# The memory's norm weights move from eight transposed blocks per row tile to the rows themselves

## The chip, the cores and the metric

The kernel runs on one core of a Trainium2 chip. The metric is the time of one execution on the device, in microseconds (us); "PE" is TensorE, "DVE" VectorE, "ACT" ScalarE, "POOL" GpSimd and "SP" SyncE, which issues most of the transfers here.

## The reference, cut to what matters

One step of a two-layer streaming encoder on 512 prompt tokens and 64 sample tokens, 1024 wide. Each layer has one input projection, three mixers side by side (stick-breaking attention, gated linear attention, latent attention), an output projection, a cross-attention into 256 memory tokens, and a feed-forward part. The change is in how the prompt's memory becomes keys and values, once per layer:

```python
def rmsnorm(x, g):
    xf = x.astype(jnp.float32)
    y = xf * lax.rsqrt(jnp.mean(xf * xf, axis=-1, keepdims=True) + NORM_EPS)
    return (y * g.astype(jnp.float32)).astype(x.dtype)

def memory_kv(mem, w):
    B, M, _ = mem.shape                              # 1, 256, 1024
    h = rmsnorm(mem, w['g_mem_norm'])
    k = rmsnorm((h @ w['w_ck']).reshape(B, M, MEM_HEADS, MEM_HD), w['g_ckn'])
    v = (h @ w['w_cv']).reshape(B, M, MEM_HEADS, MEM_HD)
    return k, v
```

## The kernel before

**Precision.** Every large product is made of three matmuls on a rounded high part and a low part of each operand (a = aH + aL, with aH the value rounded to fp32r and aL the rest): aH bH + aL bH + aH bL. Making the two parts of a block costs one rounding copy, nearly always on ACT, and one subtraction on DVE (`split_to`). So each 128x1024 piece of weights costs ACT and DVE an instruction each, and so does each block of activations.

**Stages of a layer.** The names in the profile carry a stage and the layer: `win0` is the input projection, `gla0`, `sb0` and `mlaq0`/`mlak0`/`mlap0`/`mlas0` are the gated linear, the stick-breaking and the latent attention, `wout0` holds the memory's keys and values and the output projection, `cross0` and `ffn0` follow. The stage around the change runs from about 124 to 260 us in layer 0 and from 969 to 1105 us in layer 1.

**What sets the order of the work.** Inside this stage the order of the instructions on each engine is not written out. The pieces of work are Python generators in `Order` (L732 to L797). `Order.run` picks the next piece by its rank among those whose inputs are due by a modelled clock (`Clock`, L39 to L176); attention units have rank 0, and the long projection groups ("D" groups, mostly of 24 matmuls) rank 10, so that they fill the time for which an attention unit's softmax work is modelled to last. `Clock.cost` (L89) gives each instruction a modelled length; on DVE it is, for n elements per partition,

```python
            if op in ("tensor_scalar", "tensor_copy", "memset") and not psum:
                return 0.07 + n / 1920
            return 0.07 + n / 960 + (0.06 if op == "scalar_tensor_tensor" else 0.0)
```

A change in the instructions of one piece thus moves other pieces too. Once written, the order on each engine is fixed: an instruction waits for the one ahead of it on its engine and for its inputs.

**An attention unit.** A stick-breaking unit of a 128-token tile (`tile_attention`) makes scores on PE (`sb0.S`), two exponential-type passes per head on ACT into `sb0.kp` and `sb0.sg`, masks on POOL, on DVE a running sum (scan) in `sb0.kp` and a combination into `sb0.sg` per head, then transposes on PE (`sb0.T<-ident,sb0.sg`), copies of those to `sb0.PT` (one head's on ACT, the other's on DVE), and the product with the values on PE (`sb0.T<-sb0.PT,win0.sbv`). The units of the third and fourth token tile and of the sample come two each. A latent query unit (`mlaq0`) is a projection, a chain of small DVE, ACT and POOL instructions (`mlaq0.j`, `mlaq0.s`), and a transpose.

**The memory.** `memory_norm` (L800) loads 256 rows as two 128x1024 tiles (`wout0.mem`), takes the sum of squares on ACT (`wout0.mj` is its unused output), forms 1/rms (`wout0.s`) and scales each tile by it, with one DVE instruction per tile. `memory_turn` (L813) transposes the sixteen 128x128 blocks on PE, four into one PSUM bank. The norm's weight is now one number per partition, since a partition is one of the 1024 features, so each block is scaled as it is split: one ACT instruction into `wout0.mH` and one DVE instruction into `wout0.mL`, 128x128 each. The weights lie in `gT`, a small table of all gains that is loaded as rows (`grow`, L339) and transposed at the start. `memory_kv` (L830) then multiplies by the key and value weights, eight D groups of 24 matmuls (`wout0.D` with 256 columns). The transposes, the scores' transposes and other small things share one ring of three PSUM banks (`T`).

Of the kernel before, what the change touches and what calls it, by code (L numbers as in the profile page):

```python
# [20 lines left out]
D = 1024  # L21
# [195 lines left out]
def tile_hybrid(ctx, tc, ins, outs):  # L217
    clock = tc.clock = Clock()
    nc = Engines(tc)
    I = ins  # L220
# [15 lines left out]
    def nm(s):  # L236
        uid[0] += 1
        return f"{phase[0]}.{s}_{uid[0]}"

    def big(dt=F32, name="b"):  # L240
        return clock.tile(bp.tile([128, BIGN], dt, tag="big", name=nm(name)), "big", 11)
# [20 lines left out]
    def pt4(name="pt"):  # L262
        return clock.tile(turn["pool"].tile([128, 1024], F32, tag="pt", name=nm(name), bufs=2), "pt", 2)

    def small(n, tag="s"):
        bufs = {"s": 8, "y": 4}.get(tag, 1)
        return clock.tile(sp.tile([128, 16 if tag == "y" else 8], F32, tag=tag, name=nm(tag), bufs=bufs), tag, bufs)[:, :n]
# [4 lines left out]
    def ps_(tag):  # L272
        return clock.tile(pp.tile([128, 512], F32, tag=tag, name=nm(tag), bufs=PB[tag]), tag, PB[tag])

    def cst(shape, name, dt=F32):
        return const.tile(shape, dt, tag=name, name=name)
# [6 lines left out]
    def act(out, in_, func, **kw):  # L283
        name = TABLES.get(func)
        if name is not None and name != held["set"]:
            load = nc.scalar.preload_act_table_set(name).ins
            for i in held["users"]:
                behind(tc, load, i)
            held.update(set=name, load=load, users=[load])
        ins = nc.scalar.activation(out, in_, func, **kw).ins  # L290
        if name is not None:
            behind(tc, ins, held["load"])
            held["users"].append(ins)

    def copyA(out, in_, scale=None):
        if scale is None:
            act(out, in_, AF.Copy)
        else:
            act(out, in_, AF.Identity, scale=scale)

    def tt(out, a, b, op, eng=None):
        (eng or nc.vector).tensor_tensor(out, a, b, op=op)

    def stt(out, a, s, b, op0, op1):
        nc.vector.scalar_tensor_tensor(out, a, s, b, op0=op0, op1=op1)

    MUL, ADD, SUB = ALU.mult, ALU.add, ALU.subtract
# [18 lines left out]
    for t, (c0, n) in enumerate(TILES):  # L326
        if t == 3:
            w_first = fetch_w(I["w_in"][0, :, 768:1024], KD, 256)
        raw = big(name="xin")[:, 0:D]
# [6 lines left out]
    nc.chain.update(act=None, dve=None, pool=None)  # L336
    grow = u("kp", "grow")[0:84, 0:128]
    nc.vector.memset(grow, 1.0)
    for r0, g in ((16, "g_cross_norm"), (32, "g_ffn_norm"), (48, "g_mem_norm")):  # L339
        nc.pool_queue.dma_start(grow[r0:r0 + 16, :], I[g].rearrange("l (r c) -> (l r) c", c=128))  # L340
    nc.pool_queue.dma_start(grow[64:68, :], I["g_cq"].rearrange("l (r c) -> (l r) c", c=128))
    nc.pool_queue.dma_start(grow[68:70, :], I["b_gla_gate"])
# [38 lines left out]
    def rstd_small(ss, inv_n):  # L381
        nc.vector.tensor_scalar(ss, ss, inv_n, EPS, op0=MUL, op1=ADD)
        rows, n = ss.shape[0], ss.shape[1]
        nc.gpsimd.tensor_tensor(ss, ss, mhalf[0:rows, 0:n], op=ALU.pow)
# [49 lines left out]
    def tr(out, in_):  # L434
        n = in_.shape[0]
        nc.tensor.transpose(out, in_, ident[0:n, 0:n])
# [16 lines left out]
    def split_to(src, H, L):  # L453
        copyA(H, src)
        tt(L, src, H, SUB)
# [202 lines left out]
    gT = cst([128, 84], "gT")  # L658
# [44 lines left out]
    for t, (c0, n) in enumerate(TILES):  # L703
        if t < 3:
            x_squares(t, n)
        for i in range(0, KD, 4):
            d = ps_("DTS"[(2 * t + i // 4) % 3])
# [92 lines left out]
    def memory_norm(l, out):  # L800

        out["raw"] = big(name="mem")
        for t in range(2):
            raw, junk = out["raw"][:, t * 1024:(t + 1) * 1024], pt4("mj")
            nc.sync.dma_start(raw, I["mem_prompt"][0, t * 128:(t + 1) * 128, :])
            ss = small(1)
            act(junk, raw, AF.Square, accum_out=ss)
            rstd_small(ss, 1.0 / D)
            nc.vector.tensor_scalar(raw, raw, ss, None, op0=MUL)
        return  # L810
        yield

    def memory_turn(l, out):  # L813

        H = out["H"] = big(F32R, "mH")[:, 0:KD * MEM].rearrange("p (k c) -> p k c", c=MEM)
        L = out["L"] = big(F32R, "mL")[:, 0:KD * MEM].rearrange("p (k c) -> p k c", c=MEM)
        for t in range(2):
            for i in range(0, KD, 4):
                d = ps_("T")
                for j in range(4):  # L820
                    c = t * 1024 + (i + j) * 128
                    tr(d[:, j * 128:(j + 1) * 128], out["raw"][:, c:c + 128])
                for j in range(4):
                    g = gT[:, 48 + 8 * l + i + j:49 + 8 * l + i + j]
                    cs = slice(t * 128, (t + 1) * 128)
                    copyA(H[:, i + j, cs], d[:, j * 128:(j + 1) * 128], scale=g)
                    stt(L[:, i + j, cs], d[:, j * 128:(j + 1) * 128], g, H[:, i + j, cs], MUL, SUB)
                yield "T"

    def memory_kv(l, out, od):  # L830
# [67 lines left out]
    def layer(l, xn):  # L898
# [617 lines left out]
        if l == 0:  # L1516
# [15 lines left out]
        od.line([(["kv", "mlan"], mlas(p), None) for p in range(4)], 4, name="mlas")  # L1532
        phase[0] = f"wout{l}"
        od.line([(["glan"], memory_norm(l, mem), "mem")], 1, tag="T")
        od.line([(["mem"], memory_turn(l, mem), "memt")], 1, 0, tag="T")
        od.line([(["win", "memt"], memory_kv(l, mem, od), "memx"), (["gla", "win"], wout("gla", 256, 2), "wo1"),
                 (["sbn"], wout("sb", 0, 2), "wo0"), (["mlan"], wout("mla", 512, 4), None)], 1, 10, tag="D")
# [235 lines left out]
```

## Time and profile before

| | before |
|---|---|
| time, median of 3 runs (lowest to highest) | 1716.88 us (1714.28 to 1719.4) |
| the profiled execution's own time | 1715.26 us |
| its span | 1713.5 us |
| PE busy | 1649.6 us, 96% of the span |
| DVE busy | 1230.8 us, 72% |
| ACT busy | 903.9 us, 53% |
| mean granted clock of PE | 0.99 |

The span is what the profile covers; the execution's own time is 1.76 us more. Busy is the time in which an engine executes something. Every instruction stands under one line, L195, the helper that records them all, so groups are told apart by the names of what they write and read: `wout0.mL<-wout0.T,gT,wout0.mH` writes `wout0.mL` from a PSUM bank of the ring `T`, the gains and `wout0.mH`.

### The profile page before, as it was taken

To read this page: it belongs to the slowest core of one execution; us is meant where nothing else is said; L and a number is where in the kernel's file an instruction comes from. 1 tells how busy PE (TensorE), PEld (TensorE's weight loads), DVE (VectorE), ACT (ScalarE), POOL (GpSimd) and SP (SyncE) were. 2 spreads that over 40 slices of the span, in tenths; PEclk is the share of its full clock that TensorE was granted. 3 is DMA by queue.
4 is the path that set the end of the run, shared out by engine and by line. 5 is a ranking of instruction groups with operands and counts; after the bars stand their busy time and mean duration, and the time that the engine had idled before them with its cause. 6 is when DMAs were issued, how large, how long until landed. Compare 5 with 4: busy or idle time off the path is not lost.

```text
span 1713.5 us, 30864 instructions
## 1 busy us (share of the span) xinstructions
PE 1649.6 (96%) x12231; PEld 1532.3 (89%) x12231; DVE 1230.8 (72%) x2496; ACT 903.9 (53%) x1929; POOL 206.8 (12%) x303
## 2 busy tenths in 40 slices
PE   8999999999899999999999989999998999999998
PEld 7887887789889999999998978877897999999998
DVE  5737798776898677766657378987669986766763
ACT  6426688655654444344343456886666544334431
POOL 4323341020000000000134042400200000000000
PEclk9999999999999999999998999999999999999999
DMA  5321130022022322222222213200211233233221
GB/s 165 112 72 58 64 116 26 26 74 75 25 80 93 99 80 93 99 85 89 79 83 84 81 47 98 82 26 25 99 50 50 75 99 99 74 99 99 77 97 56
DMA packets 113647, 133.30 MB, mean 78 GB/s; under 512 B 10610, under 2 KB 95712, under 8 KB 113504
## 3 DMA queue, kind: packets, MB, share of 16 engines
q1 hardware_dynamic: 113120, 131.30, 24.2%
q8 instruction: 96, 1.57, 0.4%
q14 instruction: 47, 0.39, 0.1%
q0 software_dynamic: 352, 0.03, 0.0%
q10 hardware_dynamic: 32, 0.01, 0.0%
HBM read 123.64 MB, written 7.68 MB: 77 GB/s over the span
## 4 chain that ended last, share of the span: by engine, by line
PE 76%; DVE 13%; ACT 4%; issue 3%; POOL 2%; DMA 0%; POOLq 0%; ACTq 0%; DVEq 0%
PE ffn1.D L195 9%; PE ffn0.D L195 9%; PE ffn1.S L195 6%; PE ffn1.T L195 6%; PE ffn0.S L195 6%; PE ffn0.T L195 6%; PE win1.D L195 5%; PE win0.D L195 4%; PE cross0.D L195 3%; PE cross1.D L195 3%; PE wout1.D L195 2%; PE wout0.D L195 2%; PE cross0.T L195 1%; PE cross1.T L195 1%; PE mlap1.T L195 1%
## 5 line engine op out<-in xcount | busy, mean ns | idle before, releaser
L195 ACT ACTIVATE ffn1.wH<-ffn1.wraw 128x1024 fp32r<-128x1024 f32 x66 | 60.6, 918 | 115.8 <-PE ffn1.T L195 61.5
L195 ACT ACTIVATE ffn0.wH<-ffn0.wraw 128x1024 fp32r<-128x1024 f32 x66 | 60.6, 918 | 110.5 <-PE ffn0.T L195 60.0
L195 DVE TENSOR_TENSOR ffn1.sL<-ffn1.sum,ffn1.sH 128x1024 fp32r<-128x1024 f32 x44 | 53.7, 1221 | 40.3 <-ACT ffn1.sH L195 40.3
L195 DVE TENSOR_TENSOR ffn0.sL<-ffn0.sum,ffn0.sH 128x1024 fp32r<-128x1024 f32 x44 | 53.7, 1221 | 39.9 <-ACT ffn0.sH L195 39.8
L195 PE MATMUL ffn0.D<-cross0.bT,ffn0.sH 128*128 128x288 f32 x352 | 72.4, 297 | 2.4 <-ACT ffn0.sH L195 1.5
L195 PE MATMUL ffn1.D<-cross1.bT,ffn1.sH 128*128 128x288 f32 x352 | 73.1, 299 | 1.5 <-ACT ffn1.sH L195 0.9
L195 DVE TENSOR_TENSOR ffn0.wL<-ffn0.wraw,ffn0.wH 128x1024 fp32r<-128x1024 f32 x66 | 68.8, 1043 | 7.8 <-ACT ffn0.wH L195 7.2
L195 DVE TENSOR_TENSOR ffn1.wL<-ffn1.wraw,ffn1.wH 128x1024 fp32r<-128x1024 f32 x66 | 68.8, 1043 | 7.8 <-ACT ffn1.wH L195 7.3
L195 PE MATMUL ffn1.S<-cross1.bT,ffn1.sH 128*128 128x288 f32 x352 | 72.6, 297 | 1.0 <-ACT cross1.bT L195 0.5
L195 PE MATMUL ffn0.S<-cross0.bT,ffn0.sH 128*128 128x288 f32 x352 | 71.9, 294 | 0.8 <-ACT cross0.bT L195 0.5
L195 POOL TENSOR_TENSOR ffn0.u<-ffn0.u,ffn0.u 128x576 f32<-128x576 f32 x6 | 10.0, 1664 | 469.5 <-DVE ffn0.wL L195 462.5
L195 ACT ACTIVATE ffn1.sH<-ffn1.sum 128x1024 fp32r<-128x1024 f32 x44 | 46.3, 1055 | 27.1 <-PE ffn1.S L195 22.9
L195 PEld LDWEIGHTS ffn0.D<-cross0.bT,ffn0.sH 128*128 128x128 f32 x352 | 56.7, 189 | 4.0 <-ACT ffn0.sH L195 1.9
L195 ACT ACTIVATE ffn0.sH<-ffn0.sum 128x1024 fp32r<-128x1024 f32 x44 | 46.3, 1055 | 26.0 <-PE ffn0.S L195 22.8
L195 PEld LDWEIGHTS ffn1.D<-cross1.bT,ffn1.sH 128*128 128x128 f32 x352 | 57.3, 191 | 2.9 <-ACT ffn1.sH L195 1.3
L195 PEld LDWEIGHTS ffn1.S<-cross1.bT,ffn1.sH 128*128 128x128 f32 x352 | 57.6, 191 | 1.7 <-ACT cross1.bT L195 0.8
L195 PEld LDWEIGHTS ffn0.S<-cross0.bT,ffn0.sH 128*128 128x128 f32 x352 | 57.0, 189 | 1.4 <-ACT cross0.bT L195 0.8
L195 PE MATMUL ffn1.D<-cross1.bT,ffn1.sL 128*128 128x288 f32 x176 | 52.6, 299 | 0.0
L195 PE MATMUL ffn1.S<-cross1.bT,ffn1.sL 128*128 128x288 f32 x176 | 52.5, 299 | 0.0
L195 PE MATMUL ffn0.D<-cross0.bT,ffn0.sL 128*128 128x288 f32 x176 | 52.4, 298 | 0.0
L195 PE MATMUL ffn0.S<-cross0.bT,ffn0.sL 128*128 128x288 f32 x176 | 52.2, 297 | 0.0
L195 ACT ACTIVATE ffn0.part<-ffn0.D 128x288 f32<-128x288 f32 x66 | 26.9, 408 | 41.7 <-PE ffn0.D L195 41.7
(875 smaller groups left out, 6458.6 us busy)
## 6 DMA issues: line engine op xcount, KB each, us to landing
ffn0.wraw<-in_w_gate_dram SPq DMA_DIRECT2D x11, 1024.0 KB, 5.3
ffn0.wraw<-in_w_up_dram SPq DMA_DIRECT2D x11, 1024.0 KB, 5.5
ffn0.wraw<-in_w_down_dram SPq DMA_DIRECT2D x11, 1024.0 KB, 5.0
ffn1.wraw<-in_w_gate_dram SPq DMA_DIRECT2D x11, 1024.0 KB, 5.3
ffn1.wraw<-in_w_up_dram SPq DMA_DIRECT2D x11, 1024.0 KB, 5.4
ffn1.wraw<-in_w_down_dram SPq DMA_DIRECT2D x11, 1024.0 KB, 5.0
win1.wraw<-in_w_in_dram SPq DMA_DIRECT2D x7, 1024.0 KB, 5.3
win0.wraw<-in_w_in_dram SPq DMA_DIRECT2D x6, 1024.0 KB, 5.7
```

The source lines that it names most:

```text
L195: r = fn(*args, **kw)
```

## The change

The norm's weights are loaded per layer as one row broadcast over 128 partitions (`mg`, 128x1024), and applied to the memory's rows in the instruction that applies 1/rms. That instruction now has two tensor inputs. After the transposing nothing is left to scale, so the four blocks of a bank are split at once: one rounding copy on ACT and one subtraction on DVE, 128x4x128 each. The weights' load into `grow` goes.

```diff
-    for r0, g in ((16, "g_cross_norm"), (32, "g_ffn_norm"), (48, "g_mem_norm")):
+    for r0, g in ((16, "g_cross_norm"), (32, "g_ffn_norm")):
         nc.pool_queue.dma_start(grow[r0:r0 + 16, :], I[g].rearrange("l (r c) -> (l r) c", c=128))
...
         out["raw"] = big(name="mem")
+        gb = pt4("mg")
+        nc.sync.dma_start(gb, I["g_mem_norm"][l:l + 1, :].broadcast_to([128, D]))
         for t in range(2):
...
             rstd_small(ss, 1.0 / D)
-            nc.vector.tensor_scalar(raw, raw, ss, None, op0=MUL)
+            stt(raw, raw, ss, gb, MUL, MUL)
...
-                for j in range(4):
-                    g = gT[:, 48 + 8 * l + i + j:49 + 8 * l + i + j]
-                    cs = slice(t * 128, (t + 1) * 128)
-                    copyA(H[:, i + j, cs], d[:, j * 128:(j + 1) * 128], scale=g)
-                    stt(L[:, i + j, cs], d[:, j * 128:(j + 1) * 128], g, H[:, i + j, cs], MUL, SUB)
+                cs = slice(t * 128, (t + 1) * 128)
+                split_to(d.rearrange("p (k c) -> p k c", c=128), H[:, i:i + 4, cs], L[:, i:i + 4, cs])
```

The function that it calls is there already:

```python
    def split_to(src, H, L):
        copyA(H, src)
        tt(L, src, H, SUB)
```

Since `Order.run` works by the modelled lengths, the order of the whole stage comes out another way, in both layers alike. Three places show it.

On DVE, from the scaling of the second memory tile to the first stick-breaking scans (`win0.wL` are low parts of input weights, `win0.G` a gate; a scan stands here as a SCALAR_TENSOR_TENSOR on `sb0.kp`); first before, then the change:

```order
L195 TENSOR_SCALAR wout0.mem_1490<-wout0.mem_1490,wout0.s_1500 128x1024
L195 SCALAR_TENSOR_TENSOR win0.G_282<-win0.G_282,gT,gla0.u_1454 128x576
L195 SCALAR_TENSOR_TENSOR wout0.mL_1506<-wout0.T_1507,gT,wout0.mH_1505 128x128
L195 TENSOR_TENSOR win0.wL_1554<-win0.wraw_1547,win0.wH_1553 128x1024
L195 SCALAR_TENSOR_TENSOR wout0.mL_1506<-wout0.T_1507,gT,wout0.mH_1505 128x128
L195 TENSOR_TENSOR win0.wL_1825<-win0.wraw_1822,win0.wH_1824 128x1024
```

```order
L195 SCALAR_TENSOR_TENSOR wout0.mem_1489<-wout0.mem_1489,wout0.s_1501,wout0.mg_1490 128x1024
L195 SCALAR_TENSOR_TENSOR win0.G_281<-win0.G_281,gT,gla0.u_1453 128x576
L195 TENSOR_TENSOR wout0.mL_1507<-wout0.T_1508,wout0.mH_1506 128x4x128
L195 TENSOR_TENSOR win0.wL_1549<-win0.wraw_1542,win0.wH_1548 128x1024
L195 TENSOR_TENSOR win0.wL_1802<-win0.wraw_1799,win0.wH_1801 128x1024
L195 TENSOR_TENSOR win0.G_281<-win0.D_1552,in.R_140 128x288
```

One subtraction stands where four stood, and they no longer alternate with the 128x1024 subtractions.

On PE, at the third group of memory transposes, between the scores of the second token tile and its successor's filler; first before, then the change:

```order
L195 MATMUL sb0.S_1671<-win0.sbk_278,win0.qo_276 128x256
L195 MATMUL sb0.S_1671<-win0.sbk_278,win0.qo_277 128x256
L195 MATMUL sb0.T_1686<-ident,sb0.sg_1591 128x128 x2
L195 MATMUL sb0.T_1690<-ident,sb0.sg_1605 128x128 x2
L195 MATMUL wout0.T_1694<-ident,wout0.mem_1490 128x128 x4
L195 MATMUL win0.D_1707<-in.hH_135,win0.wH_1553 128x288
```

```order
L195 MATMUL sb0.S_1660<-win0.sbk_277,win0.qo_275 128x256
L195 MATMUL sb0.S_1660<-win0.sbk_277,win0.qo_276 128x256
L195 MATMUL wout0.T_1674<-ident,wout0.mem_1489 128x128 x4
L195 MATMUL sb0.T_1682<-ident,sb0.sg_1593 128x128 x2
L195 MATMUL sb0.T_1686<-ident,sb0.sg_1607 128x128 x2
L195 MATMUL win0.D_1690<-in.hH_134,win0.wH_1548 128x288
```

The memory's transposes move ahead of the unit's two; at the fourth group they move from behind the third tile's first scores to ahead of them.

On PE, behind the scores of the first unit of the third token tile (128x384) and one D group of 24 (its last row is the first here); first before, then the change:

```order
L195 MATMUL win0.D_1832<-win0.wH_1828,in.hL_138 128x256
L195 MATMUL sb0.T_1796<-sb0.PT_1795,win0.sbv_279 64x128 x8
L195 MATMUL sb0.S_1874<-win0.sbk_278,win0.qo_277 128x384
L195 MATMUL sb0.S_1886<-win0.sbk_278,win0.qo_277 128x384
L195 MATMUL sb0.T_1899<-ident,sb0.sg_1774 128x128 x3
L195 MATMUL sb0.T_1904<-ident,sb0.sg_1786 128x128 x3
L195 MATMUL win0.T_1909<-ident,win0.j_1857 128x128 x2
L195 MATMUL win0.D_1916<-win0.wH_1824,in.hH_135 128x256
```

```order
L195 MATMUL win0.D_1809<-win0.wH_1805,in.hL_137 128x256
L195 MATMUL sb0.T_1842<-ident,sb0.sg_1764 128x128 x3
L195 MATMUL sb0.T_1847<-ident,sb0.sg_1776 128x128 x3
L195 MATMUL sb0.T_1786<-sb0.PT_1785,win0.sbv_278 64x128 x8
L195 MATMUL sb0.S_1862<-win0.sbk_277,win0.qo_276 128x384
L195 MATMUL sb0.S_1874<-win0.sbk_277,win0.qo_276 128x384
L195 MATMUL sb0.T_1842<-sb0.PT_1841,win0.sbv_278 64x128 x6
L195 MATMUL win0.T_1893<-ident,win0.j_1834 128x128 x2
L195 MATMUL sb0.S_1900<-win0.sbk_277,win0.qo_275 128x512
L195 MATMUL sb0.S_1912<-win0.sbk_277,win0.qo_275 128x512
L195 MATMUL win0.D_1924<-win0.wH_1801,in.hH_134 128x256
```

The unit's transposes come sooner behind its scores, its product with the values follows with only the next unit's scores in between, and the next tile's scores stand ahead of the next D group instead of behind it. Through the rest of the stick-breaking units it goes on so: they end with one D group of the memory's keys and values among them where five stood, and the other four stand among the latent query and key units instead.

## Rows read from the trace of the kernel before

**Rows 1.** Windows: busy us (x count) of PE, PEld, DVE, ACT, POOL; clock; DMA.

```profile
124.00:260.00 136.00, 124.89 (x959) 109.79 (x959) 105.50 (x276) 94.82 (x239) 47.83 (x84) 0.99 0.25 83
969.00:1105.00 136.00, 124.21 (x965) 108.80 (x964) 105.53 (x274) 94.48 (x239) 48.12 (x84) 1.00 0.26 83
```

**Rows 2.** What PE waited for, 124 to 260 us: total us, times, longest us.

```profile
PE mlaq0.T L195 <- POOL mlaq0.j L195: 3.6, 6, 1.5
PE sb0.T L195 <- DVE sb0.PT L195: 2.6, 2, 1.9
PE win0.T L195 <- DVE sb0.PT L195: 1.4, 1, 1.4
PE wout0.T L195 <- DVE wout0.mL L195: 1.0, 1, 1.0
PE wout0.T L195 <- ACT win0.qo L195: 1.0, 1, 1.0
PE sb0.T L195 <- DVE wout0.mL L195: 0.4, 1, 0.4
```

**Rows 3.** The same from 969 to 1105 us.

```profile
PE wout1.T L195 <- DVE wout1.mL L195: 1.0, 1, 1.0
```

**Rows 4.** Tile `wout0.mH`, ns min/median/max, first and last start; who waited.

```profile
L195 ACT ACTIVATE wout0.mH<-wout0.T,gT x16: 349/367/417, 134.4 to 165.0; 128x128 fp32r<-128x128 f32 x16
L195 DVE SCALAR_TENSOR_TENSOR wout0.mL<-wout0.T,gT,wout0.mH x16: 319/344/352, 134.8 to 166.1; 128x128 fp32r<-128x128 f32 x16
...
  ACT wout0.mH L195: 12.7, 8
```

**Rows 5.** Timeline of PE: start, us, instruction, [idle before].

```profile
157.84 0.36 PE L195 MATMUL win0.D<-win0.wH,in.hH 128*128 128x256 f32 x1
...
160.89 0.43 PE L195 MATMUL sb0.T<-sb0.PT,win0.sbv 128*64 128x128 f32 x2
163.18 1.09 PE L195 MATMUL sb0.T<-sb0.PT,win0.sbv 128*64 128x128 f32 x14 [1.86 <-DVE sb0.PT L195]
```

**Rows 6.** Timeline of DVE, the same place.

```profile
159.42 2.18 DVE L195 TENSOR_TENSOR_SCAN sb0.kp<-sb0.kp,zero 128x384 f32<-128x384 f32 x2
...
162.44 0.68 DVE L195 COPY sb0.PT<-sb0.T 128x512 f32<-128x512 f32 x1
```

**Rows 7.** Window of 10 us, columns as in rows 1.

```profile
160.00:170.00 10.00, 8.14 (x58) 6.52 (x57) 7.79 (x16) 4.36 (x14) 3.44 (x7) 0.83 0.01 2
```

**Rows 8.** Groups by shape on ACT, 124 to 260 us: busy us, mean ns.

```profile
L195 ACT ACTIVATE sb0.PT<-sb0.T 128x512 f32<-128x512 f32 x3 | 1.9, 623 | 0.0
```

**Rows 9.** The same on DVE.

```profile
L195 DVE TENSOR_TENSOR wout0.wL<-wout0.wraw,wout0.wH 128x1024 fp32r<-128x1024 f32 x11 | 13.4, 1217 | 2.5 <-ACT wout0.wH L195 2.4
...
L195 DVE TENSOR_TENSOR X<-X,wout0.D 128x288 f32<-128x288 f32 x11 | 4.7, 445 | 0.6 <-PE wout0.D L195 0.6
...
L195 DVE COPY sb0.PT<-sb0.T 128x512 f32<-128x512 f32 x5 | 3.4, 677 | 0.3 <-PE sb0.T L195 0.3
...
L195 DVE SCALAR_TENSOR_TENSOR win0.G<-win0.G,gT,gla0.u 128x576 f32<-128x576 f32 x2 | 1.6, 814 | 0.7 <-ACT gla0.u L195 0.7
```

**Rows 10.** Tile `wout0.mem`.

```profile
L195 DVE TENSOR_SCALAR wout0.mem<-wout0.mem,wout0.s x2: 752/752/753, 129.2 to 133.0; 128x1024 f32<-128x1024 f32 x2
...
DMA to landing us min/median/max: 3.7/4.1/4.5
```

**Rows 11.** Timeline of SP, 85 to 101 us.

```profile
93.14 1.57 SPq L195 DMA_DIRECT2D out_dram<-gla0.s  x2
```

**Rows 12.** Timeline of PE, one unit of the fourth tile.

```profile
171.35 1.13 PE L195 MATMUL sb0.S<-win0.sbk,win0.qo 64*128 64x512 f32 x4
```

**Rows 13.** Timeline of DVE, the same unit.

```profile
174.91 0.76 DVE L195 TENSOR_TENSOR sb0.sg<-sb0.sg,sb0.kp 128x511 f32<-128x511 f32 x1
175.59 1.30 DVE L195 TENSOR_TENSOR_SCAN sb0.kp<-sb0.kp,zero 128x512 f32<-128x512 f32 x1
...
177.27 0.68 DVE L195 TENSOR_TENSOR sb0.sg<-sb0.sg,sb0.kp 128x511 f32<-128x511 f32 x1
```

## The prediction

> **What bounds the kernel now.** I read the windows by stage first, then the waits of PE inside the stage that the change touches, then the two tiles that it makes in another way. In the windows [rows 1], after the stretch and its length, PE is busy 124.89 of 136 us in layer 0 and 124.21 in layer 1: some 11 to 12 us per layer are idle PE, and no more than that can be won, since the change leaves the matmuls as they are. DVE has 105.5 us of work there and ACT 94.8; neither is full, but their work comes in bursts between which PE has to have something else to do. The waits [rows 2] say what PE stood still for: 2.4 us of it is at the memory's turning (1.0 for `wout0.mL`, 1.0 for a bank behind `win0.qo`, 0.4 for a unit's transposes behind `wout0.mL`), 4.0 us for copies of stick-breaking weights (2.6 and 1.4 for `sb0.PT` on DVE), and 3.6 us for the latent queries. Layer 1 repeats them, as its 1.0 us on `wout1.mL` shows [rows 3]. So 2.4 us per layer hang on the edited lines, and 7.6 us on units that the change only moves.
>
> **The work removed and added.** Per layer ACT has sixteen roundings of 0.367 us, 5.9 us, and DVE sixteen subtractions of 0.344 us, 5.5 us; the roundings waited 12.7 us, eight times, behind those subtractions [rows 4], which is nothing on PE by itself but keeps a PSUM bank of the ring of three in use. In the change four ACT copies of 512 elements take their place; the nearest row, a copy of 512 from PSUM, is 0.623 us [rows 8], so 2.5 us: ACT gains 3.4 us. The four subtractions of 512 from PSUM stand in no row. They lie between 0.445 us (288 elements from PSUM) and 1.217 us (1024 elements in SBUF), and a one-source copy of 512 from PSUM took 0.677 us [rows 9]; a line through the first two gives 0.445 + 224 x (1.217 - 0.445)/736 = 0.68, so I take 0.68, four of them 2.7 us. DVE gains 2.8 us there, and between 0.6 and 3.7 by the bounds.
>
> Against that, the scaling of the rows gets a second tensor. Before it is 0.752 us for 1024 elements [rows 10]. The same kind of instruction with two tensors took 0.814 us for 576; at the slope of the line above 1024 make 0.814 + 448 x 0.00105 = 1.28 us. Its floor is that 0.814, and its ceiling twice it, 1.63. Two per layer cost DVE 1.06 us more (0.1 to 1.8). DVE's net gain is 2.8 - 1.06 = 1.8 us per layer (between -1.2 and +3.6).
>
> [...]
>
> **The new load.** `mg` is 512 KB per layer on SP's queue. A memory tile of that size landed in 4.1 us [rows 10]. In the changed order it stands between the two stores of `gla0.s`, which were issued from 93.1 us on [rows 11], and the first scaling that needs it was at 129.2 us [rows 10]: 36 us of cover, so I cost it at nothing; without the cover it would be 4.1 us. Behind it on SP stand the second of those stores and the stores of `win0.kn`, for which nobody waits. It takes one of two buffers of the ring that `mj` and the weights' copies share, until the second scaling; the first stick-breaking copies stand behind it in the order. The gain's row that is no longer loaded on POOL's queue at the start is on no wait of PE: nothing.
>
> **What the new order does.** The PE waits at the memory go: one copy and one subtraction free a bank that eight instructions held, and the last two groups of transposes come ahead of unit transposes rather than behind them. I take all of it, -2.4 us per layer.
>
> The stick-breaking units get closer. In the change the first unit of the third tile has eight transposes and one D group between its scores and its own transposes. A D group of 24 took from 157.84 to 160.89, 3.05 us [rows 5], and eight transposes at that pace 1.0, so 4.05 us; its second head is wanted three transposes later, at 4.4. What a unit needs is shown by one of the fourth tile: scores from 171.35 to some 172.4 [rows 12], the first head's combination done at 175.67, the second's at 177.95 [rows 13], or 3.3 and 5.5 us after the scores, with a copy in between. With scans of 1.09 us [rows 6] instead of 1.30 and as much off the other steps it is some 4.8 for 384 elements; a gate product of about 0.8 us (the 0.814 of [rows 9]) that the new order puts between makes it 5.6. That gives a wait of 1.2 us. The two sample units have again one D group and eight small matmuls, 4.05 us, against 5.5: 1.5 us each, 3.0. Three products with the values come with only another product and scores between, some 1.7 us after their transposes (0.6 for eight matmuls at the pace of the 14 in [rows 5], 1.13 for scores [rows 12]), where a copy of 0.68 can stand behind a scan of 1.30: 1.98 - 1.7 is some 0.2 each, 0.6. The second unit of the third tile and those of the fourth have a second D group or a whole unit more between: nothing. Together 4.8 us in place of the 4.0 for `sb0.PT`: +0.8 us per layer. Its bounds are 0 (the D groups cover all of it), a gain of 4.0, and the second rival below.
>
> The four D groups that leave the stick-breaking units stand among the latent queries and keys. There they could cover part of the 3.6 us [rows 2], or be missed later; I take zero, with that 3.6 as the bound on both sides. [...]
>
> **The sum.** Per layer -2.4 + 0.8 = -1.6 us, which is near the 1.8 that DVE gains; twice, -3.2 us. From the execution of 1715.26 that is 1712.1 us; the runs' median stands 1.6 higher, at 1716.88, so I predict 1713.7 us, with 1711.7 to 1716 as this case's own range. 0.3%, or 5.15 us, is about what a measurement of this kernel can tell from no change, and the forecast lies inside it.
>
> **Rival: a larger gain.** If the D groups among the latent queries cover a quarter of their 3.6 us (0.9), and the unit waits that I count with 4.8 are half as long (2.4), a layer gains 2.4 + 4.0 - 2.4 + 0.9 = 4.9 us; two layers and the 1.7 us at the slow clock make 11.5: 1705.4 us. For it: DVE and ACT together lose 5.2 us of work per layer in a stage where PE's idle time is bursts of theirs, and banks come free sooner. Against it: the closer units.
>
> **Rival: slower.** The order is made with modelled lengths, and a scan of 512 elements, priced with 0.07 + 0.06 + 512/960 = 0.66 us, took 1.30 [rows 13]. Two heads make 1.3 us per unit that the order does not know of, and before it was D groups in plenty behind the scores that covered it. If all six units of the third and fourth tile and the sample come too early by 1.3 us, the waits are 7.8 + 0.6 = 8.4 us in place of 6.4, +2.0 per layer, and with a stretch of slow clock (1.7) in layer 1 as well, +5.7: 1722.6 us. It decides from 1.5 us of wait per unit on (9.0 against 6.4, twice).
>
> **Rival: no effect.** ACT and DVE are idle for 30 to 40 us per layer in this stage [rows 1]; the waits at the memory only move to the next unit behind, since each unit's chain ends when it ended: 1716.9 us.
>
> **How the numbers follow.** Forecast 0.35, larger gain 0.34, no effect 0.17, slower 0.14. The larger gain counts as faster by over 0.3%, and so do 0.02 of the forecast: 0.36. The rest of the forecast and no effect are 0.50, slower 0.14. The range reaches from 1704 us, the larger gain with some more of the 3.6 us, to 1721, which leaves out the worst half of the slower case and the tail beyond the larger gain.
>
> **What would show it.** Right: four `mL` instructions of 0.6 to 0.75 us, two `mem` scalings of 1.2 to 1.35, DVE 1.5 to 2 us less busy per layer in the stage, no PE wait for `mL`, and PE waits for `sb0.sg` of 1 to 1.5 us at the third tile's first unit and the sample's. Wrong: PE waits of 2 us or more at every unit, a wait for `mg`, latent-query waits far from 3.6 us, or a slow clock in other places.

## The result, and the profile after

The changed kernel takes 1730.73 us (median of 4 runs, 1726.22 to 1731.65) against 1716.12 for the kernel before: 1.0072 times as long, with a 95% interval of 1.0054 to 1.009. It is slower by 0.7%, outside the range I gave, and beyond the 1722.6 us of the slower rival. The profiled execution is the quickest of the four, 1726.22 us with a span of 1724.5 and a mean clock of 0.989. The other three have 0.985 to 0.987, so the profile below shows 11 of the 14.6 us and not all of them.

The windows of [rows 1] in the changed kernel:

```profile
124.00:260.00 136.00, 123.13 (x922) 105.33 (x921) 100.27 (x259) 91.41 (x232) 51.65 (x85) 0.99 0.25 81
969.00:1105.00 136.00, 123.66 (x935) 106.27 (x935) 96.23 (x243) 88.00 (x218) 49.93 (x83) 0.99 0.23 75
```

In layer 0 DVE and ACT are busy for 5.2 and 3.4 us less than before, and PE not for longer but for 1.8 us less. Part of that is work that now comes later: the window holds 922 matmuls, where it held 959. POOL is busy for longer, though the change gives it no work. A stretch with the same work in both kernels reaches from the last matmul of the gated linear attention to the last of the cross-attention (columns as in [rows 1]; first before, then the change):

```profile
130.06:467.76 337.70, 319.72 (x2362) 275.48 (x2362) 260.88 (x672) 229.76 (x601) 61.08 (x100) 0.99 0.18 58
975.74:1312.29 336.55, 317.82 (x2363) 273.69 (x2363) 260.70 (x673) 229.67 (x600) 61.38 (x100) 0.99 0.18 59
```

```profile
130.37:473.15 342.78, 323.08 (x2364) 275.60 (x2363) 259.24 (x661) 225.30 (x589) 64.03 (x100) 0.99 0.18 58
980.71:1323.23 342.52, 323.14 (x2363) 275.33 (x2363) 258.71 (x661) 225.66 (x589) 63.00 (x100) 0.99 0.18 58
```

Here DVE is busy for 1.6 and 2.0 us less per layer, as forecast, and the stretch is 5.1 and 6.0 us longer: all of the 11 us lie in it. What the new instructions cost, by tile (ns min/median/max):

```profile
L195 ACT ACTIVATE wout0.mH<-wout0.T x4: 577/594/622, 134.7 to 155.4; 128x512 fp32r<-128x512 f32 x4
L195 DVE TENSOR_TENSOR wout0.mL<-wout0.T,wout0.mH x4: 659/687/691, 135.3 to 156.3; 128x512 fp32r<-128x512 f32 x4
...
L195 DVE SCALAR_TENSOR_TENSOR wout0.mem<-wout0.mem,wout0.s,wout0.mg x2: 1285/1286/1287, 129.3 to 133.3; 128x1024 f32<-128x1024 f32 x2
...
L195 SPq DMA_DIRECT2D wout0.mg<-in_g_mem_norm_dram x1: 1262/1262/1262, 93.9 to 93.9; - x1
```

These are the prices of the prediction: 0.69 us (0.68), 1.29 (1.28), and a load issued at 93.9 us, 35 us ahead of the first scaling. The loss is elsewhere. What PE waited for in the stage, to set beside [rows 2], and below it the first line of layer 1:

```profile
PE mlaq0.T L195 <- POOL mlaq0.j L195: 7.0, 6, 2.8
PE sb0.T L195 <- DVE sb0.sg L195: 3.0, 2, 1.5
PE sb0.T L195 <- ACT win0.qo L195: 0.9, 1, 0.9
PE wout0.T L195 <- DVE wout0.u L195: 0.8, 2, 0.5
PE wout0.D L195 <- DVE wout0.wL L195: 0.4, 1, 0.4
...
PE mlaq1.T L195 <- POOL mlaq1.j L195: 6.7, 8, 2.8
```

No line for `wout0.mL` is left, and the 4.0 us for `sb0.PT` have become 3.0 for `sb0.sg`. New are 0.8 us in front of the transposes of the memory's keys (`wout0.u`). But the latent queries, which I had put at their old 3.6 us, cost 7.0. The timelines of POOL, DVE and PE in the changed kernel show how; in brackets the idle time ahead:

```profile
223.68 2.78 DVE L195 TENSOR_TENSOR wout0.wL<-wout0.wraw,wout0.wH 128x1024 fp32r<-128x1024 f32 x2
223.77 2.94 POOL L195 TENSOR_TENSOR mlaq0.j<-mlaq0.j,mlaq0.s 64x256 f32<-64x256 f32 x2 [2.62 <-ACT wout0.wH L195]
226.76 0.43 PE L195 MATMUL mlaq0.T<-ident,mlaq0.j 64*96 64x64 f32 x4 [1.65 <-POOL mlaq0.j L195]
...
229.93 0.97 POOL L195 TENSOR_TENSOR mlaq0.j<-mlaq0.j,mlaq0.s 128x256 f32<-128x256 f32 x2 [1.10 <-ACT mlaq0.y L195]
...
236.03 1.95 POOL L195 TENSOR_TENSOR mlaq0.j<-mlaq0.j,mlaq0.s 128x256 f32<-128x256 f32 x2 [0.93 <-DVE mlaq0.s L195]
236.35 1.37 DVE L195 TENSOR_TENSOR wout0.wL<-wout0.wraw,wout0.wH 128x1024 fp32r<-128x1024 f32 x1 [0.40 <-ACT wout0.wH L195]
...
239.06 3.89 POOL L195 TENSOR_TENSOR mlaq0.j<-mlaq0.j,mlaq0.s 128x256 f32<-128x256 f32 x2
240.26 1.21 DVE L195 TENSOR_TENSOR wout0.wL<-wout0.wraw,wout0.wH 128x1024 fp32r<-128x1024 f32 x1
241.47 1.21 DVE L195 TENSOR_TENSOR mlak0.wL<-mlak0.wraw,mlak0.wH 128x1024 fp32r<-128x1024 f32 x1
...
243.00 0.88 PE L195 MATMUL mlaq0.T<-ident,mlaq0.j 128*96 128x128 f32 x3 [2.78 <-POOL mlaq0.j L195]
```

Each query unit ends in two products on POOL, which rescale `mlaq0.j`. Six of the ten pairs of layer 0 take 0.96 to 1.08 us, and one 1.50, beside a DVE instruction of 1.12 us on `sb0.u`. The other three, beside which DVE runs a subtraction of 128x1024 for a weight's low part, take 2.94, 1.95 and 3.89 us, and end just behind the subtractions. DVE pays too: the second subtraction of the first meeting, which started at 224.82 us, takes 1.64 us and the one at 236.35 takes 1.37, where 1.21 to 1.23 is usual. Three such meetings cost POOL 2.0 + 1.0 + 2.9 = 5.9 us, and PE's waits behind them are 1.65, 0.51 and 2.78 us. In the kernel before there were two, of 2.23 and 1.99 us; its timelines, at the first of them and at an undisturbed pair:

```profile
232.01 2.23 POOL L195 TENSOR_TENSOR mlaq0.j<-mlaq0.j,mlaq0.s 128x256 f32<-128x256 f32 x2 [0.16 <-issue]
232.78 1.21 DVE L195 TENSOR_TENSOR wout0.wL<-wout0.wraw,wout0.wH 128x1024 fp32r<-128x1024 f32 x1
...
244.05 0.97 POOL L195 TENSOR_TENSOR mlaq0.j<-mlaq0.j,mlaq0.s 128x256 f32<-128x256 f32 x2 [0.55 <-DVE mlaq0.s L195]
```

The subtractions are there because the order changed: the memory's key and value groups, whose weights DVE splits into `wout0.wH` and `wout0.wL`, come in pairs with one set of weights, and of the five groups that stood among the stick-breaking units four now stand among the latent queries and keys. Behind the 2.8 us wait the granted clock is 0.83 for 10 us, in both layers (windows of the changed kernel):

```profile
240.00:250.00 10.00, 7.22 (x38) 6.12 (x38) 4.19 (x11) 3.20 (x12) 4.45 (x5) 0.83 0.46 141
1090.00:1100.00 10.00, 7.22 (x40) 6.12 (x39) 4.32 (x11) 3.30 (x12) 4.67 (x5) 0.83 0.46 140
```

But the kernel before had such stretches in other places, one of them in [rows 7]; the mean clock of the two profiled executions is 0.990 and 0.989, so the clock is at most a small part of the 11 us.

### The profile page after: what moved, and what is told of

It is laid out like the page before. It is cut to its first block, busy times and chain, and to the rows that moved or that the text cites. A ratio compares the mean times of both kernels' runs of the same rounds, so it can differ in the third digit from the quotient of the medians.

```text
span 1724.5 us, 30839 instructions
## 1 busy us (share of the span) xinstructions
PE 1657.9 (96%) x12231; PEld 1533.9 (89%) x12231; DVE 1228.2 (71%) x2472; ACT 896.3 (52%) x1905; POOL 209.8 (12%) x302
## 4 chain that ended last, share of the span: by engine, by line
PE 79%; DVE 10%; ACT 4%; POOL 2%; issue 2%; DMA 1%; POOLq 0%; ACTq 0%; DVEq 0%
PE ffn0.D L195 9%; PE ffn1.D L195 9%; PE ffn0.S L195 6%; PE ffn1.S L195 6%; PE ffn0.T L195 6%; PE ffn1.T L195 6%; PE win1.D L195 5%; PE win0.D L195 4%; PE cross0.D L195 3%; PE cross1.D L195 3%; PE wout0.D L195 3%; PE wout1.D L195 3%; PE mlap1.T L195 1%; PE mlap0.T L195 1%; PE cross1.T L195 1%
```

## The experiments

My theory was: the instructions do what was forecast, the order that comes with them costs more than they give, and the dearest part of it is the meeting of POOL's products with DVE's subtractions. The rivals: the instructions themselves cost time, and the stick-breaking units wait because the order prices scans too low. Several kernels replay an order instead of making it. The picks of one kernel are kept as a list, and the two lines of `Order.run` that choose are replaced:

```diff
-                now = max(clock.pe + SLACK, min(at(x) for x in free))
-                x = min((x for x in free if at(x) <= now), key=lambda x: (x["rank"], at(x), x["n"]))
+                n = next(self.picks)
+                x = next(x for x in free if x["n"] == n)
```

Each ratio is to runs of the kernel before on the same chip.

| kernel | median, us | to the kernel before (95%) |
|---|---|---|
| the change | 1730.73 | 1.0072 (1.0054 to 1.009) |
| 1: its instructions, order of before | 1711.39 | 0.9964 (0.9951 to 0.9977) |
| 2: instructions of before, its order | 1743.29 | 1.0152 (1.0127 to 1.0176) |
| 3: the change, query products on DVE | 1719.84 | 1.0015 (1.0002 to 1.0029) |
| 4: the change, weight splits with one source | 1732.22 | 1.0086 (1.007 to 1.0103) |
| 5: before, SLACK 0.05 | 1721.52 | 1.0032 (1.0021 to 1.0042) |
| 6: the change, scans priced as measured | 1710.18 | 0.997 (0.9958 to 0.9981) |
| 7: the turning alone, order of before | 1711.27 | 0.9972 (0.9961 to 0.9984) |
| 8: the scaling and load alone, order of before | 1714.98 | 0.9994 (0.9983 to 1.0005) |
| 9: as 1, query products on DVE | 1710.93 | 0.9968 (0.9955 to 0.998) |
| 10: as 6, query products on DVE | 1708.68 | 0.9953 (0.994 to 0.9967) |

**1. The change's instructions in the order of before** (the replay, with the picks of before).

> All of the change's instructions, but the pieces of work are picked in the order that the kernel before picked them (the picks are read from a list). Theory 'order': the loss comes from where the pieces stand, so it goes: PE waits for mlaq0.j back to about 3.6 us per layer, no mL waits (2.4 us in before), time 1711 to 1717 us, so ratio to before 0.997 to 1.0. Rival 'edited instructions' (the two-tensor scaling, one instruction per bank, the mg load cost by themselves): the time stays with the change, 1726 to 1732 us, ratio about 1.007.

It is faster, by 0.36%, so in this order the instructions cost nothing, and time and query waits came as forecast. Its waits in the stage are those of [rows 2] without the two for `wout0.mL`, and with 0.6 us instead of 1.0 behind `win0.qo`:

```profile
PE mlaq0.T L195 <- POOL mlaq0.j L195: 3.9, 7, 1.5
PE sb0.T L195 <- DVE sb0.PT L195: 2.6, 2, 1.9
PE win0.T L195 <- DVE sb0.PT L195: 1.4, 1, 1.4
PE wout0.T L195 <- ACT win0.qo L195: 0.6, 1, 0.6
```

**2. The instructions of before in the change's order** (the same replay, with the change's picks).

> The kernel before, with its pieces picked in the order of the change. Theory 'order': it is slow as well, mlaq0.j waits of 6 to 7 us per layer, and DVE has 1.8 us more work per layer: 1727 to 1736 us, ratio 1.006 to 1.012. Rival 'edited instructions': it stays at 1714 to 1719 us, ratio 1.0.

With the old instructions the new order costs 1.5%, more than the 1727 to 1736 us of the forecast. It takes over the latent-query waits whole, gets a wait on the sixteen-part turning that the change's own instructions don't have, and runs at a lower clock for some 50 us. Waits, and then the window:

```profile
PE mlaq0.T L195 <- POOL mlaq0.j L195: 6.8, 8, 2.8
PE sb0.T L195 <- DVE wout0.mL L195: 1.9, 1, 1.9
```

```profile
160.00:210.00 50.00, 46.46 (x322) 34.93 (x320) 29.95 (x52) 25.75 (x69) 15.06 (x30) 0.80 0.04 13
```

By an estimate, the length times what the clock lacks to 1.00, these 50 us lose 10 us at 0.80, and 1020 to 1070 us lose 8.5 at 0.83. The changed kernel has no stretches of that length, so the 1.5% is not what the order costs it: that is the distance from kernel 1 to the change, 1.08 points or some 18 us.

**3. The change with the query products on DVE**, its order kept.

```diff
-                tt(q3[:, :, 0:64], q3[:, :, 0:64], s[:, 0:4].unsqueeze(2).broadcast_to([rn, 4, 64]), MUL, nc.gpsimd)
-                tt(qf, qf, s[:, 4:8].unsqueeze(2).broadcast_to([rn, 4, 32]), MUL, nc.gpsimd)
+                tt(q3[:, :, 0:64], q3[:, :, 0:64], s[:, 0:4].unsqueeze(2).broadcast_to([rn, 4, 64]), MUL)
+                tt(qf, qf, s[:, 4:8].unsqueeze(2).broadcast_to([rn, 4, 32]), MUL)
```

> The change in its own order of pieces, with the two rescaling products at the end of each latent query unit on DVE instead of POOL. Theory 'exclusion' (POOL's product of two SBUF tensors and DVE's 1.2 us subtraction of two SBUF tensors do not run at once, so POOL's 0.4 us become 1.4 to 3.2): with nothing on POOL to be held up, PE waits for mlaq0.j fall from 7.0 to at most 4 us per layer and the time by 4 to 8 us, to 1721 to 1727 us, although DVE has some 7 us more work per layer. Rival 'queue' (the units wait because DVE has too much queued in front of their small instructions): DVE gets more, the waits stay at 7 us or grow, time 1730 us or more.

Two products per unit, moved to an engine that has more work, take 0.57 points of the ratio away, 9.8 us, and the time is below the forecast. The waits:

```profile
PE sb0.T L195 <- DVE sb0.sg L195: 3.0, 2, 1.5
PE mlaq0.T L195 <- DVE mlaq0.j L195: 2.3, 4, 0.6
PE wout0.D L195 <- DVE wout0.wL L195: 1.7, 4, 0.8
```

7.0 us became 2.3, while DVE's weights come 1.3 us later: 4.7 - 1.3 = 3.4 per layer, and twice that is 6.8. The two profiled executions are 6.6 us apart (1726.22 and 1719.63). The low clock behind the wait is gone (1.00 from 200 to 250 us), but the stretch from 460 to 480 us has 0.83 where it had 0.91, so the clock adds nothing to these 6.6. The medians' 9.8 us are more; the changed kernel's other executions are slower than its profiled one and have a lower clock (0.985 to 0.987 against 0.989), and what lowered it there no profile shows.

**4. The change with weight splits that read one tensor.** The low part of the memory's key and value weights is made from `wH` alone, with a row sum, so that it takes as long but reads one tensor; the memory's keys and values are then others than the reference's.

```diff
-            tt(L, raw[:, ks, cs], H, SUB, nc.gpsimd if between and i else None)
+            if one:
+                nc.vector.tensor_scalar(L, H, 2.0 ** -13, None, op0=MUL, op1=ADD, accum_out=small(1))
+            else:
+                tt(L, raw[:, ks, cs], H, SUB, nc.gpsimd if between and i else None)
...
-                w = load_w(I[name][l, :, c * 256:(c + 1) * 256], KD, 256, by="k")
+                w = split_w(fetch_w(I[name][l, :, c * 256:(c + 1) * 256], KD, 256), "k", one=True)
```

> The change in its own order of pieces; the low parts of the memory's key and value weights are no longer raw minus rounded (two SBUF tensors) but the rounded part times a constant with a row sum (one SBUF tensor), so these low parts, and with them the memory's keys and values, are not the reference's. Theory 'exclusion': POOL's rescaling products under these instructions take their 0.4 and 0.6 us, where they took 1.4 to 3.2 (except under mlak0.wL, which stays a subtraction); mlaq0.j waits fall to 4 us per layer or less, time 4 to 8 us below the change. If the new instruction is of half the length some of that is DVE's relief, and the lengths on POOL decide. Rival 'queue': the lengths on POOL stay and so do the waits, unless the new instruction is shorter.

This tells a busy DVE from one that reads two tensors. A product pair that runs under such a split, in the timeline (DVE, then POOL):

```profile
239.29 1.21 DVE L195 TENSOR_SCALAR_CACHE_REDUCE wout0.wL<-wout0.wH 128x1024 fp32r<-128x1024 f32 x1
239.53 0.97 POOL L195 TENSOR_TENSOR mlaq0.j<-mlaq0.j,mlaq0.s 128x256 f32<-128x256 f32 x2 [0.59 <-DVE mlaq0.s L195]
```

The twenty products as a group (ns min/median/max), and the waits of PE in the stage:

```profile
L195 POOL TENSOR_TENSOR mlaq0.j<-mlaq0.j,mlaq0.s x20: 392/560/613, 214.4 to 254.3; 128x256 f32<-128x256 f32 x8, 128x128 f32<-128x128 f32 x8, 64x256 f32<-64x256 f32 x2, 64x128 f32<-64x128 f32 x2
```

```profile
PE wout0.D L195 <- DVE wout0.wL L195: 4.2, 2, 3.6
PE mlaq0.T L195 <- POOL mlaq0.j L195: 3.5, 5, 0.8
```

With 1.21 us on DVE as before, no product is stretched: the longest takes 0.613 us, where the same group in the changed kernel is 394/614/3196 ns. PE's wait is back at 3.5. As a saving of time it failed: the forecast was 4 to 8 us less than the change, but there is a wait of 4.2 us for weights, and there are stretches of low clock (0.54 from 190 to 200 us, 0.66 from 220 to 230) that the change doesn't have. So this run bears out the theory of the two tensors (3.196 us against 0.613) and says nothing of the price.

**5. Before with another order** (`SLACK = 0.1` to `0.05`).

> The kernel before, every instruction of it, with one number of the order's rule changed: the slack with which a piece counts as due is 0.05 instead of 0.1. In its order no D group of the memory's keys and values stands before the end of the stick-breaking units, where five stood (one in the change). Theory 'order': packing the units that close costs by itself, whatever brings it about: 1725 to 1745 us, ratio 1.005 to 1.015, with PE waits for sb0.sg or sb0.PT of over 4 us and for mlaq0.j of over 5 us per layer. Rival: the close order is bad only together with the change's or the old turning instructions in it, 1713 to 1720 us.

The premise was false. Its order has the same five groups among the stick-breaking units, and differs by small moves. It is nevertheless 0.3% slower, with a mean clock of 0.984 in the profile against 0.99. I did not find why; it shows only that small moves of the order can cost some 5 us.

**6. The change with the scan's price as measured.**

```diff
-            return 0.07 + n / 960 + (0.06 if op == "scalar_tensor_tensor" else 0.0)
+            return 0.27 + n * 0.002 if op == "tensor_tensor_scan" else 0.07 + n / 960 + (0.06 if op == "scalar_tensor_tensor" else 0.0)
```

> The change with one modelled length set right: a scan is priced with 0.27 + 0.002 n us (1.04 for 384, 1.29 for 512, as measured) in place of 0.07 + n/960. The picks are its own. Theory: the close units come from underpriced scans, so with the right price PE waits for sb0.sg (3.0 us per layer in the change) fall below 1.5, two D groups stand among the units again, and the time is 1712 to 1722 us. Rival: the order is a draw that no single price governs, the loss lies with the latent queries' collisions on POOL, which the price does not know; mlaq0.j waits stay at 6 us or more and the time at 1724 us or more.

DVE's `sb0.sg` is gone from the waits, and the kernel is 0.3% faster than before and a full point faster than the change. Neither side of the forecast came whole: the time is 2 us below the theory's range, and the rival's waits came without its time. Where the gain lies is not clear, since the order changes ahead of the stage as well: the last products of the gated linear attention start at 116.7 us in place of 120.3, and from there to the last matmul of the cross-attention it takes 2.4 us longer, with one more D group of 24 in between; at that last matmul it is 1.3 us ahead of the kernel before in layer 0 (466.5 against 467.8 us) and 4.4 in layer 1. And the latent queries still wait (waits of this kernel in layer 0):

```profile
PE mlaq0.T L195 <- POOL mlaq0.j L195: 7.2, 9, 2.0
PE sb0.T L195 <- DVE win0.cT L195: 1.1, 1, 1.1
```

**7 and 8. Half of the change each, in the order of before**, shown against the change. In 7 the turning alone:

```diff
-        gb = pt4("mg")
-        nc.sync.dma_start(gb, I["g_mem_norm"][l:l + 1, :].broadcast_to([128, D]))
...
-            stt(raw, raw, ss, gb, MUL, MUL)
+            nc.vector.tensor_scalar(raw, raw, ss, None, op0=MUL)
```

> Picks of the kernel before; of the change only the turning, one copy and one subtraction per bank. The norm's weights are left out altogether, so memory keys and values are not the reference's. If the gain of 6 us in the run with the old order is the memory's waits and DVE's relief at the turning, this has all of it and the scaling's 1.06 us per layer more: 1708 to 1712 us, ratio 0.994 to 0.997. If it came from the start (one load less) or elsewhere, 1715 to 1718 us.

In 8 the scaling and the load alone, with sixteen plain splits:

```diff
-                split_to(d.rearrange("p (k c) -> p k c", c=128), H[:, i:i + 4, cs], L[:, i:i + 4, cs])
+                for j in range(4):
+                    split_to(d[:, j * 128:(j + 1) * 128], H[:, i + j, cs], L[:, i + j, cs])
```

> Picks of the kernel before; of the change only the scaling of the rows with the weights (two-tensor instruction and the mg load); the sixteen blocks are split one by one as before, without a scale. The waits for mL (1.4 us and the 1.0 for a bank per layer) stay, and DVE has 1.06 us more: 1716 to 1720 us, ratio 0.999 to 1.002. If the load or the two-tensor form cost more than the sum had it (a wait on mg, POOL held up), over 1721 us.

The turning brings 0.28%, 4.8 us, and the scaling with its load nothing that the measurement tells from zero. Both times are within about 1 us of their forecasts.

**9 and 10. The query products on DVE, where the order is another**: the edit of 3 in kernel 1 and in kernel 6, with the order of each kept.

> The change's instructions with the picks of the kernel before, and the two rescaling products of each latent query unit on DVE instead of POOL. In this order only two of twenty products per layer are held up (1.65 and 1.4 us instead of 0.4), and DVE is nearly full in that stretch (30 of 32 us). If what moving them is worth is the collisions alone, there is little to win here and DVE's 6 us more per layer cost something: 1710 to 1717 us against 1711.4 with POOL. If moving them is good in any order (POOL is simply slow), 1704 to 1708 us.

> The change with the right scan price (its picks kept) and the two products on DVE. There PE waits 7 us per layer for mlaq0.j, as in the change's own order. By the collisions these fall below 3 us and the time from 1710.2 to 1700 to 1706 us, below every kernel so far. If the 7 us there are the units' own latency, they stay, now on DVE, and the time is 1708 us or more.

In the order of before the edit is worth nothing (0.9968 against 0.9964). In that of 6 it takes the wait for the queries from 7.2 to 1.7 us in layer 0, as much as in kernel 3, but the ratio only from 0.997 to 0.9953, some 3 us; the two intervals overlap, and the forecast of 1700 to 1706 us was missed. Kernel 10 has the lowest median of all, 0.5% below the kernel before, but its interval overlaps those of 1, 6, 7 and 9. Its longest waits:

```profile
PE wout0.D L195 <- DVE wout0.wL L195: 1.9, 4, 1.1
PE mlaq0.T L195 <- DVE mlaq0.j L195: 1.7, 2, 1.1
```

## Why the prediction was wrong

**The instructions: right.** The prices were met, nobody waited for the load, and no wait for `mL` was left. The forecast of -2.4 us per layer for the memory's waits is 4.8 in all; in the order of before kernel 7 gains 4.8 (its interval is 2 us to either side), and kernel 1, with all of the change, 6.2. In the changed order less of it came: 0.9 us behind `win0.qo` now stand at a unit's transposes, and the 0.8 for `wout0.u` were in no term. The second tensor took the scaling from 0.752 us [rows 10] to 1.286, 1.7 times as long.

**The stick-breaking units: the place right, the size small.** I forecast 4.8 us in place of 4.0, with 1.2 at the third tile's first unit. The changed kernel has 3.0 for `sb0.sg` and 0.9 for `win0.qo`, so about 3.9; the wait at that unit is 1.46 us, and the other, of 1.54 at 185.10 us, is that of the sample's first unit. The sample's second, forecast at 1.5 as well, has none:

```profile
161.68 0.52 PE L195 MATMUL sb0.T<-ident,sb0.sg 128*128 128x128 f32 x3 [1.46 <-DVE sb0.sg L195]
...
185.10 0.66 PE L195 MATMUL sb0.T<-ident,sb0.sg 128*128 128x128 f32 x4 [1.54 <-DVE sb0.sg L195]
```

The term was +0.8 and came out at about zero. The slower rival named scans that are priced too low, and kernel 6 shows that pricing them right takes these waits away. But they cost what the old waits cost, 3.9 us against the 8.4 that the rival needs: it had the sign and a source of the bad order right, and not the way in which that order costs time.

**The latent queries: the step that failed.** I wrote of the four D groups that move there: "I take zero, with that 3.6 as the bound on both sides". The wait grew by 3.4 us in layer 0 and 3.1 in layer 1 in place of zero, near the end of that bound. I had asked what the groups' matmuls could cover on PE. I hadn't asked what comes with a group on the other engines, which is two subtractions of 1.22 us on DVE for each pair of groups [rows 9], beside products on POOL. The products' own rows in the trace of before, 0.4 to 1.65 us for the same shapes, were the sign that I passed over.

Kernel 4 shows that it is this: where DVE's work of equal length (1.21 us) reads one tensor, the longest product takes 0.613 us instead of 3.196. Its price in the changed order rests on kernel 3 alone: moving the products off POOL gives 9.8 us back, and kernel 9 shows that the move gives nothing in an order where only two milder meetings stand (kernel 1, whose longest product takes 1.652 us). In the order of kernel 6 a wait that falls by as much brought some 3 us (10), so the price is one of this order. Such a meeting would have been a rival for this change, and I had not weighed it.

**What is left.** In ratios to the kernel before, the instructions bring -0.36 points, the meetings on POOL and DVE +0.57, and the rest of the order +0.51, some 9 us: that is the distance from kernel 1 to kernel 3. It lies between the last matmul of the gated linear attention and the last of the cross-attention. In that stretch kernel 3 and then kernel 9 have, in both layers:

```profile
133.73:472.45 338.72, 322.17 (x2362) 274.92 (x2362) 259.67 (x681) 224.79 (x589) 55.02 (x80) 0.99 0.18 58
978.16:1316.52 338.36, 321.56 (x2363) 274.51 (x2363) 259.95 (x681) 224.72 (x589) 54.92 (x80) 0.99 0.18 58
```

```profile
134.37:468.67 334.30, 319.33 (x2362) 274.96 (x2362) 260.20 (x681) 226.66 (x589) 49.59 (x80) 0.99 0.18 59
976.26:1310.26 334.00, 319.62 (x2363) 274.98 (x2363) 260.01 (x681) 226.74 (x589) 49.48 (x80) 0.99 0.18 59
```

That is 4.4 us in each layer. Of it 1.6 and 2.4 us are idle PE, where the weights' low parts (1.7 us per layer in kernel 3) come late. The other 2.8 and 1.9 us stand as busy PE with the same matmuls, with no group of them that stands out. The change itself shows more of this: against the kernel before, its two stretches together have 2.4 us more of idle PE, since the longer waits for the queries are partly made up for by the shorter ones at the memory, and 8.7 us more of busy PE. The prediction's sum counts waits alone and has no term for that, so beside the term for the queries it lacked one. Nor has it one for the granted clock. The 1.7 us that both rivals add for a slow clock are an estimate from [rows 7], 10 us x (1 - 0.83), and no run shows them as lost time: the changed kernel has 0.83 over 10 us in each layer, behind the wait for the queries, and a mean clock of 0.989 where the kernel before has 0.990. As the ends of matmuls are modelled in the profile, time for which PE stood still can be hidden in its busy time. What makes these 8.7 us stays open.

## What to carry to other kernels

Where an edit changes modelled lengths, split it before judging it: replay the old order with the new instructions and the new order with the old. Here the edit gave 6 us and the order took some 18. The waits that a profile lists need not add up to the loss; compare a stretch with the same work in both kernels. When a block of work moves to another stage, look at what it brings for every engine, and above all for two-tensor subtractions on DVE that will stand beside short POOL products on a chain that PE waits for (here three meetings, and 7.0 us of waits where there were 3.6). A model that prices each engine alone does not see such a pair, and putting right the price of one kind of instruction took a full point off the changed kernel's ratio, though the waits for the queries stayed.

## What the runs showed of the hardware that I had not expected

A POOL product of 0.4 to 0.6 us becomes one of up to 3.196 us beside a DVE subtraction of two SBUF tensors, and keeps its length (0.39 to 0.61 us, kernel 4) beside a one-tensor instruction of the same 1.21 us. Who holds up whom is not one-sided. The third meeting by single instructions, in the changed kernel:

```profile
239.06 0.73 POOL L195 TENSOR_TENSOR mlaq0.j<-mlaq0.j,mlaq0.s 128x256 f32<-128x256 f32 x1
239.24 0.57 DVE L195 TENSOR_SCALAR mlaq0.s<-mlaq0.s 64x8 f32<-64x8 f32 x1
239.75 3.20 POOL L195 TENSOR_TENSOR mlaq0.j<-mlaq0.j,mlaq0.s 128x128 f32<-128x128 f32 x1
```

The first product was under way when a short DVE instruction started, which ended just behind it and took 0.57 us; the other nine of that kind and length in this layer take 0.15 to 0.17. The second product started ahead of both subtractions, at 240.26 and 241.47, which took their usual 1.21 us, and it ended at 242.95, behind them. So POOL started first both times, and the first time it was the DVE instruction that was drawn out, to 0.57 us, the second time POOL's product, to 3.20, as far as POOL's spans, which are rough, can tell. The runs don't show what decides between the two.
